# One decoder block on one core: the router's hand-written order, the place of the gate2 rows and the load of final_g

## Chip, cores and metric

The kernel runs on 1 core of one Trainium2 chip. The metric is the device time of one launch in microseconds (us), less is better. The core has five instruction queues that run beside each other: PE (TensorE; its weight loads are listed as PEld), DVE (VectorE), ACT (ScalarE), POOL (GpSimd) and SP (SyncE, here only an issuer of DMAs).

## What is computed

256 tokens of width 1024 go through a mixing layer (two kinds of attention), a hierarchical mixture of experts and a last RMSNorm, all in float32. The part that matters here is the second half:

```python
x = x + gate1 * (merged @ w_out[l])
h2 = rmsnorm(x, norm2_g[l]) * (1.0 + scale2) + shift2
y = hierarchical_moe(h2, router_group_w[l], ...)     # top-1 of 4 groups, then top-2 of its 4 experts
x = x + gate2 * y
return rmsnorm(x, final_g)
```

There are 16 experts (gate and up: 1024x512 each, down: 512x1024). The vectors shift, scale and gate come from a small product with the conditioning vector.

## The kernel before

The 256 tokens are two token tiles of 128 (t = 0, 1); a row of 1024 is two halves of 512 (n = 0, 1). Names as (t, n) below.

**w_out and the router.** `wo_steps` accumulates `merged @ w_out` in PSUM. For the second half (n = 1) tile 0 is finished first, tile 1 some microseconds later. `x1_half(t, n)` (L943) does three DVE operations that add the residual and an ACT square that gives the row sum `ss2`. `rstd2(t)` makes 1/rms of it in two POOL operations (L249, L250). `h2_half` (L997, DVE) forms h2. `q_transpose` (L956) transposes on PE and copies out with ACT. `token_logits` (L916, PE) and `fold` (L905: a copy of the logits out of PSUM, then a small PE matmul) give the router logits, `weigh_logits` (L1022, DVE) finishes them in `lg`. h2 is kept as a high part (`h2_hi`, L1009, an ACT cast to fp32r) and a low part (`h2_lo`, L1012, DVE). `seed` (L986, PE) puts the residual into the four output accumulators `oacc`. From `lg`, nine small DVE operations make `selb`, three small PE matmuls `rk` (L1085 to L1087) rank the tokens of each expert, DVE makes `pos` and the `onehot` selection, and `gather` (L1212) is 32 PE matmuls that collect each expert's tokens. `keep_clock` (L171) issues PE matmuls whose result nobody reads.

The order of all this on PE, DVE and ACT is what the text of the program says: it stands in a `manual_schedule` block, where each of these engines takes its instructions in the order in which they are written, and an engine whose next instruction waits does nothing else.

**Experts.** They run in 8 pairs. For a pair: 32 `gps` matmuls (gate), 32 `ups` (up), silu and product on ACT and DVE, `slot_weights`, `act_transpose`, and the `dps` matmuls (down) of the pair before; `weigh` scales the result by `adaacc[5]`, the rows of gate2, and `scatter` adds it to `oacc` by a matmul. In pair 0 `mod_rows(5)` (L472, two PE matmuls and two ACT copies) spreads the gate2 rows over the partitions. Weights are streamed by DMAs on SP's queue into 1 MB tiles of a ring; a DMA waits until PE has read the tile that it replaces.

**End.** After the last pair's `gps` and `ups`, `final_row` (L1132) spreads `final_g` over the partitions: a DMA of 4 KB into `fgrow` (L1129, ACT's queue, issued in the router), 8 matmuls of 8 rows in PE (16 instructions) and two ACT copies into `fg`. Then come the scatter of pair 6, the down matmuls and scatters of pair 7 in three column parts (`PARTS`: 512, 256 and 256 columns), and `norm_part` for each. `norm_end` (L1166) adds the sums of squares of both token tiles, takes the power -1/2 on POOL, scales on ACT and DVE, and writes the result in four DMAs of 256 KB, two from ACT's queue and two from SP's.

Of the kernel before, what the change touches and what calls it, by code (L numbers as in the profile page):

```python
# [13 lines left out]
ALU = mybir.AluOpType  # L14
# [3 lines left out]
P = 128  # L18
# [43 lines left out]
def hybrid_block_kernel(  # L62
# [409 lines left out]
    def mod_rows(which):  # L472

        for j in range(2):
            ps = psa(f"bc{which}{j}")
            if which == 5:
                PE.matmul(ps, ones, adaacc[which, j], start=True, stop=True)
            else:
                for i, part in enumerate(msplit[which][j]):
                    PE.matmul(ps, selr if (which, j) in ON_PE else onesr, part, start=(i == 0),  # L480
                              stop=(i == 1))
            if which == 4:
                V.scalar_tensor_tensor(adaacc[4, j], ps, 1.0, norm2[0][:, 512 * j:512 * j + 512],
                                       op0=ALU.add, op1=ALU.mult)
            else:
                S.copy(adaacc[which, j], ps)
# [601 lines left out]
    h2_lo(0, 1)  # L1088
    keep_clock(4)
# [38 lines left out]
    fgrow = small.tile([P, P], F32, name="fgrow", tag="lgs")[0:KD, :]  # L1128
    nc.scalar.dma_start(fgrow, final_g.rearrange("(k p) -> k p", p=P))  # L1129
    fg = []  # L1130

    def final_row():  # L1132

        fg.append(st.tile("fg")[:, 0:D])
        for n in range(2):
            ps = psa(f"fg{n}")
            for k in range(4):
                PE.matmul(ps[:, k * P:(k + 1) * P],
                          ident[0:KD, 4 * n + k:4 * n + k + 1].broadcast_to([KD, P]), fgrow,
                          start=(k == 0), stop=True, skip_group_check=True)  # L1140
            S.copy(fg[0][:, 512 * n:512 * n + 512], ps)

    norm = {}

    def norm_part(i):
# [7 lines left out]
        for t in range(NT):  # L1153
# [3 lines left out]
            if c is not PARTS[-1]:  # L1157
                V.tensor_tensor(o[:, t, c], oacc[t][n][:, cs], fg[0][:, c], op=ALU.mult)
# [7 lines left out]
    def norm_end():  # L1166
        o, ss = norm["o"], norm["ss"]
        c, cs = PARTS[-1], slice(PARTS[-1].start - FW, FW)
        r = small.tile([P, NT], F32, name="rstdf", tag="rstd")
        V.tensor_tensor(r, ss[:, len(PARTS) - 1, :], ss[:, len(PARTS) - 2, :], op=ALU.add)  # L1170
        G.tensor_tensor(r, r, mhalf, op=ALU.pow)
        for t in range(NT):
            rt_ = r[:, t:t + 1]
            S.mul(o[:, t, 0:512], o[:, t, 0:512], rt_)
            V.scalar_tensor_tensor(o[:, t, c], oacc[t][1][:, cs], rt_, fg[0][:, c], op0=ALU.mult,  # L1175
                                   op1=ALU.mult)
            V.tensor_scalar(o[:, t, 512:c.start], o[:, t, 512:c.start], rt_, None, op0=ALU.mult)  # L1177
            nc.scalar.dma_start(out[t * P:(t + 1) * P, 0:512], o[:, t, 0:512])
            nc.sync.dma_start(out[t * P:(t + 1) * P, 512:], o[:, t, 512:])
# [170 lines left out]
    for n in range(2):  # L1350
        h2_lo(1, n)
# [4 lines left out]
    with tc.manual_schedule(engines={PE.engine}):  # L1356
        gather(0, 0)
        gather(0, 1)
        for p in range(NP):
# [17 lines left out]
            if p == 0:  # L1377
                mod_rows(5)
# [11 lines left out]
        final_row()  # L1390
# [16 lines left out]
    norm_end()  # L1407
# [99 lines left out]
```

## Time and profile before

| | |
|---|---|
| time, median of 3 runs | 470.38 us (468.78 to 470.97) |
| the profiled execution | 470.29 us, of which the span from first to last instruction is 468.6 us |
| busy PE / PEld / DVE / ACT / POOL | 448.2 (96%) / 281.2 / 220.6 / 160.6 / 14.7 us |
| router, from the end of w_out to the first expert matmul | about 224.9 to 240.7 us |
| expert pairs | 240.7 to 441.2 us |
| last pair's down, norm, output | 441.2 to 468.6 us |

In a row of the trace the first two numbers are the start and the length in us; then come engine, line, operation, result and operands without buffer numbers, shape and count. A bracket at the end tells how long the engine had stood idle and what ended that. A float32 matmul is two instructions, so that "x4" there are two matmuls of the program. The granted clock is that of PE, 1.00 for 2.4 GHz and 0.50 for 1.2 GHz.

### The profile page before, as it was taken

To read this page: it belongs to the slowest core of one execution; us is meant where nothing else is said; L and a number is where in the kernel's file an instruction comes from. 1 tells how busy PE (TensorE), PEld (TensorE's weight loads), DVE (VectorE), ACT (ScalarE), POOL (GpSimd) and SP (SyncE) were. 2 spreads that over 40 slices of the span, in tenths; PEclk is the share of its full clock that TensorE was granted. 3 is DMA by queue.
4 is the path that set the end of the run, shared out by engine and by line. 5 is a ranking of instruction groups with operands and counts; after the bars stand their busy time and mean duration, and the time that the engine had idled before them with its cause. 6 is when DMAs were issued, how large, how long until landed. Compare 5 with 4: busy or idle time off the path is not lost. (4 is left out here: it accounts for less than half of the span.)

```text
span 468.6 us, 6867 instructions
## 1 busy us (share of the span) xinstructions
PE 448.2 (96%) x2724; PEld 281.2 (60%) x2724; DVE 220.6 (47%) x378; ACT 160.6 (34%) x292; POOL 14.7 (3%) x51
## 2 busy tenths in 40 slices
PE   5999999999999999999899999999999999999991
PEld 1769988976889999978453345333533335333440
DVE  5558878956999964787640030031202111020332
ACT  3543686465663444363641012011201102110222
POOL 5210000000000000000100000000000000000000
PEclk9999999999999999999999999999999999999986
DMA  8999978789797979976779999999999999999502
GB/s 290 368 324 354 295 267 287 247 287 382 254 374 255 385 263 407 422 308 219 294 258 408 424 420 418 422 419 421 420 421 419 422 419 421 420 420 404 196 0 94
DMA packets 51971, 158.46 MB, mean 338 GB/s; under 512 B 6448, under 2 KB 16728, under 8 KB 40160
## 3 DMA queue, kind: packets, MB, share of 16 engines
q1 hardware_dynamic: 51568, 157.44, 87.6%
q8 instruction: 23, 0.38, 0.3%
q10 hardware_dynamic: 368, 0.55, 0.3%
q14 instruction: 12, 0.10, 0.1%
HBM read 156.93 MB, written 1.05 MB: 337 GB/s over the span
## 5 line engine op out<-in xcount | busy, mean ns | idle before, releaser
L1252 PE MATMUL gps<-g,hg 128*64 128x512 f32 x256 | 57.9, 596 | 0.0
L1252 PE MATMUL ups<-u,hg 128*64 128x512 f32 x256 | 56.6, 595 | 0.0
L1309 PE MATMUL dps<-d,aT 128*64 128x512 f32 x224 | 51.2, 598 | 0.0
L1281 DVE TENSOR_TENSOR act<-act,ups 128x512 f32<-128x512 f32 x8 | 5.5, 687 | 93.6 <-PE ups L1252 93.6
L409 PE MATMUL g_acc<-hT,wsp 128*128 128x256 f32 x384 | 48.4, 285 | 0.3 <-DVE wsp L363 0.3
L409 PEld LDWEIGHTS g_acc<-hT,wsp 128*128 128x128 f32 x384 | 46.7, 191 | 1.6 <-issue 1.0
L1252 PEld LDWEIGHTS ups<-u,hg 128*64 128x64 f32 x256 | 17.9, 137 | 35.3 <-issue 35.3
L1252 PEld LDWEIGHTS gps<-g,hg 128*64 128x64 f32 x256 | 17.4, 137 | 33.2 <-issue 32.6
L1309 PEld LDWEIGHTS dps<-d,aT 128*64 128x64 f32 x224 | 14.8, 136 | 25.4 <-issue 25.2
L446 DVE SCALAR_TENSOR_TENSOR adarow<-adaw,cact,adarow 128x512 f32<-128x512 f32 x40 | 29.6, 743 | 0.4
L1327 ACT CAST yh<-yt 128x512 fp32r<-128x512 f32 x15 | 9.3, 618 | 56.7 <-DVE yt L1323 56.7
L1267 ACT CAST sT<-st 128x256 fp32r<-128x256 f32 x8 | 3.0, 372 | 63.4 <-PE st L1264 63.4
L940 PE MATMUL wo<-wsp,mT 128*128 128x512 f32 x96 | 23.7, 400 | 0.7 <-DVE wsp L363 0.7
L878 PE MATMUL br<-oT,wsp 128*128 128x256 f32 x192 | 23.2, 282 | 0.0
L1280 ACT ACTIVATE act<-gps 128x512 f32<-128x512 f32 x8 | 4.8, 598 | 53.7 <-PE gps L1252 53.7
L878 PEld LDWEIGHTS br<-oT,wsp 128*128 128x128 f32 x192 | 23.0, 188 | 0.2 <-DVE wsp L363 0.2
L1335 DVE TENSOR_TENSOR yl<-yt,yh 128x512 fp32r<-128x512 f32 x7 | 4.8, 692 | 34.3 <-PE oacc L1343 32.4
L940 PEld LDWEIGHTS wo<-wsp,mT 128*128 128x128 f32 x96 | 17.6, 188 | 5.2 <-DVE wsp L363 1.1
L1323 DVE SCALAR_TENSOR_TENSOR yt<-dps,ws,adarow 128x512 f32<-128x512 f32 (+1 forms) x17 | 12.2, 719 | 14.3 <-PE dps L1309 8.3
L1288 DVE COPY aT<-actT 128x512 f32<-128x512 f32 x8 | 5.5, 691 | 27.0 <-PE actT L1286 27.0
L1212 PEld LDWEIGHTS hg<-onehot,h2s 128*128 128x128 f32 x128 | 15.7, 191 | 4.2 <-ACT yh L1327 2.4
L1212 PE MATMUL hg<-onehot,h2s 128*128 128x256 f32 x128 | 16.8, 287 | 1.0 <-DVE h2s L1012 0.5
(295 smaller groups left out, 679.4 us busy)
## 6 DMA issues: line engine op xcount, KB each, us to landing
g<-in_expert_w_gate SPq DMA_DIRECT2D x32, 1024.0 KB, 14.6
u<-in_expert_w_up SPq DMA_DIRECT2D x32, 1024.0 KB, 16.3
d<-in_expert_w_down SPq DMA_DIRECT2D x30, 1024.0 KB, 17.2
adaw<-in_ada_w SPq DMA_DIRECT2D x16, 1024.0 KB, 6.4
ada<-in_ada_w SPq DMA_DIRECT2D x8, 512.0 KB, 8.9
ada<-in_ada_w SPq DMA_DIRECT2D x16, 256.0 KB, 8.5
wo<-in_w_out SPq DMA_DIRECT2D x4, 1024.0 KB, 12.9
kaw<-in_w_in SPq DMA_DIRECT2D x4, 512.0 KB, 6.6
```

The source lines that it names most:

```text
L409: PE.matmul(self.acc[m // 2][:, (m % 2) * T:(m % 2 + 1) * T], w[a][:, kk, m * P:(m + 1) * P], hT[b][:, k, :], start=(k == 0 and i == 0 and ...
L446: V.scalar_tensor_tensor(acc, adaw[which, j, k // 4][:, k % 4, :], cact[:, k:k + 1], acc, op0=ALU.mult, op1=ALU.add)
L878: PE.matmul(bacc[br][m // 2][:, (m % 2) * T:(m % 2 + 1) * T], wk[a][:, 0, m * P:(m + 1) * P], oT[br][b][:, k, :], start=(k == 0 and i == 0 ...
L940: PE.matmul(acc[t][n], mT[b][:, k, t * P:(t + 1) * P], ws[k // 2][a][:, k % 2, :], start=(k == 0 and i == 0), stop=(k == KD - 1 and i == 2))
L1212: PE.matmul(ps[:, kk * T:(kk + 1) * T], h2s[t][i][:, k * P:(k + 1) * P], oh[:, t].rearrange("p e s -> p (e s)"), start=(n == 0 and kk == 0 ...
L1252: PE.matmul(ps[64 * i:64 * i + 64, :], hg[:, k, (lo + i) * CAP:(lo + i + 1) * CAP], wt[nm, p][half][i][:, k % 4, :], start=(k == 0), stop= ...
L1280: S.activation(av, in_place(gu["g", p]), AF.Silu)
L1281: V.tensor_tensor(av, av, in_place(gu["u", p]), op=ALU.mult)
L1288: V.tensor_copy(aT, ap.rearrange("p (f s) -> p f s", f=KF))
L1309: PE.matmul(ys[p, FW * n][64 * i:64 * i + 64, :], aTs[p][:, 2 * h + k, 64 * i:64 * i + 64], dt_[p, h][i][:, k, FW * n:FW * n + FW], start= ...
L1323: V.scalar_tensor_tensor(y, ps, ws, adaacc[5, n][:, cs], op0=ALU.mult, op1=ALU.mult)
L1327: S.copy(hi, y)
```

## The change

The router block is written in another order: `rstd2(0)` and the three h2 steps of (0, 0) come ahead of tile 1's `x1_half(1, 1)`; the second half of tile 0 (`h2_half(0, 1)`) comes after it; both last seeds stand behind the second fold; `keep_clock` is gone from here; three of the four low parts are made in other places. The second fold's copy is DVE's. `mod_rows(5)` moves from pair 0 to the place behind `rk`. `final_row` goes; a DMA on SP's queue, behind the last weights, reads `final_g` for all 128 partitions (512 KB). `norm_end` works by token tile, and the first half-row of tile 0 is written from SP's queue.

```diff
-    def mod_rows(which):
+    def mod_rows(which, js=(0, 1)):
...
-        S.copy(lgs[:, 0:cols.stop - cols.start], lgT[:, cols])
+        (V.tensor_copy if out == 32 else S.copy)(lgs[:, 0:cols.stop - cols.start], lgT[:, cols])
...
     x1_half(0, 1)
+    rstd2(0)
     q_transpose(0, 0)
+    h2_half(0, 0)
+    h2_hi(0, 0)
+    h2_lo(0, 0)
     wo_steps(1, ws, [(k, 1) for k in W3])
     q_transpose(0, 1)
-    rstd2(0)
-    h2_half(0, 0)
-    h2_hi(0, 0)
     q_transpose(1, 0)
+    token_logits(0)
     seed(0, 0)
-    token_logits(0)
+    fold(tok(0), 0, "lgs0")
     x1_half(1, 1)
+    rstd2(1)
+    q_transpose(1, 1)
+    seed(0, 1)
+    weigh_logits(0)
     h2_half(0, 1)
-    fold(tok(0), 0, "lgs0")
-    seed(0, 1)
-    q_transpose(1, 1)
-    weigh_logits(0)
-    rstd2(1)
-    h2_hi(0, 1)
-    h2_lo(0, 0)
     h2_half(1, 0)
-    seed(1, 0)
     token_logits(1)
     fold(tok(1), 32, "lgs1")
     h2_half(1, 1)
     h2_hi(1, 0)
+    h2_hi(0, 1)
     h2_hi(1, 1)
+    weigh_logits(1)
+    seed(1, 0)
     seed(1, 1)
-    weigh_logits(1)
-    keep_clock(3)
...
     PE.matmul(rk[:, NE:2 * NE], strictb, selv[:, 1, :], start=False, stop=True)
-    h2_lo(0, 1)
-    keep_clock(4)
+    h2_lo(1, 0)
+    mod_rows(5)
...
     one_hot(0)
-    for n in range(2):
-        h2_lo(1, n)
+    for t in range(NT):
+        h2_lo(t, 1)
...
             if p == 0:
-                mod_rows(5)
                 nmaxi = most_tokens()
...
-        final_row()
+        fg = st.tile("fg")[:, 0:D]
+        nc.sync.dma_start(fg, final_g.unsqueeze(0).broadcast_to([P, D]))
...
-        r = small.tile([P, NT], F32, name="rstdf", tag="rstd")
-        V.tensor_tensor(r, ss[:, len(PARTS) - 1, :], ss[:, len(PARTS) - 2, :], op=ALU.add)
-        G.tensor_tensor(r, r, mhalf, op=ALU.pow)
+        rs = small.tile([P, NT], F32, name="rstdf", tag="rstd")
+        last = len(PARTS) - 1
         for t in range(NT):
-            rt_ = r[:, t:t + 1]
-            S.mul(o[:, t, 0:512], o[:, t, 0:512], rt_)
-            V.scalar_tensor_tensor(o[:, t, c], oacc[t][1][:, cs], rt_, fg[0][:, c], op0=ALU.mult,
+            V.tensor_tensor(rs[:, t:t + 1], ss[:, last, t:t + 1], ss[:, last - 1, t:t + 1],
+                            op=ALU.add)
+        for t in range(NT):
+            G.tensor_tensor(rs[:, t:t + 1], rs[:, t:t + 1], mhalf[:, 0:1], op=ALU.pow)
+        for t in range(NT):
+            r = rs[:, t:t + 1]
+            S.mul(o[:, t, 0:512], o[:, t, 0:512], r)
+            V.scalar_tensor_tensor(o[:, t, c], oacc[t][1][:, cs], r, fg[:, c], op0=ALU.mult,
                                    op1=ALU.mult)
...
-            nc.scalar.dma_start(out[t * P:(t + 1) * P, 0:512], o[:, t, 0:512])
+            (nc.sync, nc.scalar)[t].dma_start(out[t * P:(t + 1) * P, 0:512], o[:, t, 0:512])
             nc.sync.dma_start(out[t * P:(t + 1) * P, 512:], o[:, t, 512:])
...
-    norm_end()
+    with tc.manual_schedule(engines={V.engine, S.engine, G.engine}):
+        norm_end()
```

The order in which three engines take their instructions shows the moves. Numbers at names tell buffers apart: `adarow_1305` and `adarow_1312` are the first and second half's shift rows, `rstd_2521` and `rstd_2560` are tile 0 and tile 1 before, `rstd_2491` and `rstd_2551` after.

DVE in the router, before, from the first `h2_half` to the last `weigh_logits`:

```order
L997 SCALAR_TENSOR_TENSOR h2a<-h2a,rstd_2521,adarow_1305 128x512
L947 TENSOR_TENSOR h2a<-wo_2446,adarow_793 128x512
L948 TENSOR_TENSOR xs<-xs,h2a 128x512
L950 TENSOR_TENSOR h2a<-xs,adarow_1228 128x512
L997 SCALAR_TENSOR_TENSOR h2a<-h2a,rstd_2521,adarow_1312 128x512
L1022 SCALAR_TENSOR_TENSOR lg<-lgp,rstd_2521,cb 128x20
L1012 TENSOR_TENSOR h2s_2325<-h2a,h2s_2324 128x512
L997 SCALAR_TENSOR_TENSOR h2a<-h2a,rstd_2560,adarow_1305 128x512
L997 SCALAR_TENSOR_TENSOR h2a<-h2a,rstd_2560,adarow_1312 128x512
L1022 SCALAR_TENSOR_TENSOR lg<-lgp,rstd_2560,cb 128x20
```

The same stretch of DVE with the change:

```order
L997 SCALAR_TENSOR_TENSOR h2a<-h2a,rstd_2491,adarow_1305 128x512
L1012 TENSOR_TENSOR h2s_2325<-h2a,h2s_2324 128x512
L947 TENSOR_TENSOR h2a<-wo_2446,adarow_793 128x512
L948 TENSOR_TENSOR xs<-xs,h2a 128x512
L950 TENSOR_TENSOR h2a<-xs,adarow_1228 128x512
L1022 SCALAR_TENSOR_TENSOR lg<-lgp,rstd_2491,cb 128x20
L997 SCALAR_TENSOR_TENSOR h2a<-h2a,rstd_2491,adarow_1312 128x512
L997 SCALAR_TENSOR_TENSOR h2a<-h2a,rstd_2551,adarow_1305 128x512
L908 COPY lgs_2574<-lgT 128x128
L997 SCALAR_TENSOR_TENSOR h2a<-h2a,rstd_2551,adarow_1312 128x512
L1022 SCALAR_TENSOR_TENSOR lg<-lgp,rstd_2551,cb 128x20
```

The low part of (0, 0) (L1012) now stands ahead of tile 1's residual (L947 to L950), tile 0's second `h2_half` behind it, and the second logits copy (L908) is DVE's.

PE before, from the last seed's end to the gather: the second `keep_clock` stands between `rk` and the first gather matmul.

```order
L1085 LDWEIGHTS strictb
L1085 MATMUL rk<-rt_selb,strictb 128x16
L1086 LDWEIGHTS onesb
L1086 MATMUL rk<-rt_selb,onesb 128x16
L1087 LDWEIGHTS strictb
L1087 MATMUL rk<-rt_selb,strictb 128x16
L171 LDWEIGHTS identb
L171 MATMUL warm<-identb 128x512
```

PE with the change, from the second fold to the gather:

```order
L910 MATMUL lgp<-fold_115,lgs_2574 128x20
L986 MATMUL oacc_2582<-xs,ident 128x512
L986 MATMUL oacc_2584<-xs,ident 128x512
L1084 LDWEIGHTS strictb
L1084 MATMUL rk<-rt_selb,strictb 128x16
L1085 LDWEIGHTS onesb
L1085 MATMUL rk<-rt_selb,onesb 128x16
L1086 LDWEIGHTS strictb
L1086 MATMUL rk<-rt_selb,strictb 128x16
L477 MATMUL bc_2605<-adarow_1597,onesr 128x512
L477 MATMUL bc_2608<-adarow_1608,onesr 128x512
L1200 MATMUL hg_2642<-onehot_2613,h2s_2324 128x256
```

Two seeds stand where `keep_clock(3)` stood and the gate2 rows (L477) where `keep_clock(4)` stood; the gather is now L1200.

SP's queue behind the last weights, before and then with the change:

```order
L1242 DMA d_1_3657<-in_expert_w_down 128x4x256
L1242 DMA d_1_3658<-in_expert_w_down 128x4x256
L1410 TENSOR_LOAD nmaxi
L1410 ISA x2
L1179 DMA out<-o 128x512 x2
```

```order
L1230 DMA d_1_3646<-in_expert_w_down 128x4x256
L1230 DMA d_1_3647<-in_expert_w_down 128x4x256
L1378 DMA fg<-in_final_g 128x1024
L1399 TENSOR_LOAD nmaxi
L1399 ISA x2
L1166 DMA out<-o 128x512
L1167 DMA out<-o 128x512 x2
```

SP has the load of `fg` in front of its last steps and three of the four output DMAs instead of two.

## Rows read from the trace of the kernel before

**Rows 1.** Waits of PE from 241 us on: engine, line, releaser, total, times, longest.

```profile
PE oacc L1343 <- DVE o L1158: 0.7, 1, 0.7
```

**Rows 2.** Windows: window, length, busy of PE, PEld, DVE, ACT, POOL; clock, DMA share, GB/s.

```profile
330.00:440.00 110.00, 110.00 (x535) 44.52 (x535) 18.10 (x26) 13.92 (x32) 0.00 (x0) 1.00 1.01 413
```

**Rows 3.** Timeline of the router, DVE, ACT and POOL.

```profile
223.62 0.75 DVE L997 SCALAR_TENSOR_TENSOR h2a<-h2a,rstd,adarow 128x512 f32<-128x512 f32 x1 [1.15 <-POOL rstd L250]
224.96 0.69 DVE L947 TENSOR_TENSOR h2a<-wo,adarow 128x512 f32<-128x512 f32 x1 [0.58 <-PE wo L940]
...
225.87 1.16 ACT L1009 CAST h2s<-h2a 128x512 fp32r<-128x512 f32 x1
...
226.41 0.69 DVE L950 TENSOR_TENSOR h2a<-xs,adarow 128x512 f32<-128x512 f32 x1
...
228.03 0.27 ACT L908 COPY lgs<-lgT 128x128 f32<-128x128 f32 x1
...
228.60 0.56 POOL L250 TENSOR_TENSOR rstd<-rstd,mhalf 128x1 f32<-128x1 f32 x1
...
228.94 1.08 DVE L1012 TENSOR_TENSOR h2s<-h2a,h2s 128x512 fp32r<-128x512 f32 x1
229.93 1.42 DVE L997 SCALAR_TENSOR_TENSOR h2a<-h2a,rstd,adarow 128x512 f32<-128x512 f32 x2
...
232.47 0.24 DVE L1022 SCALAR_TENSOR_TENSOR lg<-lgp,rstd,cb 128x20 f32<-128x20 f32 x1 [1.12 <-PE lgp L910]
```

**Rows 4.** Timeline of the router, PE alone.

```profile
229.54 0.60 PE L956 MATMUL qT<-ident,h2a 128*128 128x128 f32 x4
...
234.23 0.18 PE L1085 MATMUL rk<-rt_selb,strictb 128*128 128x16 bf16 x1 [0.20 <-DVE rt_selb L1080]
...
235.77 0.78 PE L1212 MATMUL hg<-onehot,h2s 128*128 128x256 f32 x3 [0.43 <-DVE onehot L1194]
237.08 3.73 PE L1212 MATMUL hg<-onehot,h2s 128*128 128x256 f32 x29 [0.53 <-DVE h2s L1012]
240.74 7.09 PE L1252 MATMUL gps<-g,hg 128*64 128x512 f32 x32
```

**Rows 5.** Timeline of pair 0 behind its last `ups` matmul.

```profile
254.84 0.69 DVE L1281 TENSOR_TENSOR act<-act,ups 128x512 f32<-128x512 f32 x1 [13.53 <-PE ups L1252]
...
255.27 1.96 PE L477 MATMUL bc<-adarow,onesr 128*128 128x512 f32 x4
257.18 0.60 PE L1286 MATMUL actT<-ident,act 128*128 128x128 f32 x4
```

**Rows 6.** Timeline of PE and DVE where the last pair's down begins.

```profile
437.66 3.65 PE L1309 MATMUL dps<-d,aT 128*64 128x512 f32 x16
...
441.14 0.69 DVE L1330 TENSOR_TENSOR yl<-yt,yh 128x512 fp32r<-128x512 f32 x1 [0.74 <-ACT yh L1327]
...
441.25 2.05 PE L1138 MATMUL fg<-fgrow,ident 8*128 8x128 f32 x16
443.22 0.73 PE L1343 MATMUL oacc<-yh,sT 128*128 128x512 f32 x2
...
444.38 5.26 PE L1297 MATMUL dps<-d,aT 128*64 128x512 f32 x16
```

**Rows 7.** Windows around that place, columns as in rows 2.

```profile
440.50:444.00 3.50, 3.50 (x23) 2.53 (x20) 1.44 (x2) 1.81 (x4) 0.00 (x0) 1.00 0.01 4
444.50:447.50 3.00, 3.00 (x8) 0.88 (x10) 0.69 (x1) 0.00 (x0) 0.00 (x0) 0.50 0.00 0
```

**Rows 8.** Timeline of the end.

```profile
458.47 0.20 ACT L1155 ACTIVATION_READ_ACCUMULATOR act<-oacc 128x1 f32 x1
...
459.20 0.16 DVE L1170 TENSOR_TENSOR rstdf<-ssf 128x2 f32<-128x2 f32 x1 [1.29 <-ACT act L1155]
459.44 0.70 POOL L1171 TENSOR_TENSOR rstdf<-rstdf,mhalf 128x2 f32<-128x2 f32 x1 [230.29 <-DVE rstdf L1170]
...
460.95 1.01 SPq L1179 DMA_DIRECT2D out<-o  x2
```

More of the change, by code (lines that the diff above doesn't have):

```diff
@@ L470, in mod_split @@
             msplit[which].append((hi, lo))
-    def mod_rows(which):
-        for j in range(2):
+    def mod_rows(which, js=(0, 1)):
+        for j in js:
             ps = psa(f"bc{which}{j}")
@@ L1127, in hybrid_block_kernel @@
     PARTS = [slice(0, 512), slice(512, 768), slice(768, 1024)]
[L1128 to L1134, printed above, removed]
-        for n in range(2):
[L1136 to L1141, printed above, removed]
     norm = {}
@@ L1157, in norm_part @@
             if c is not PARTS[-1]:
-                V.tensor_tensor(o[:, t, c], oacc[t][n][:, cs], fg[0][:, c], op=ALU.mult)
+                V.tensor_tensor(o[:, t, c], oacc[t][n][:, cs], fg[:, c], op=ALU.mult)
         if c is not PARTS[-1]:
@@ L1168, in norm_end @@
         c, cs = PARTS[-1], slice(PARTS[-1].start - FW, FW)
-        r = small.tile([P, NT], F32, name="rstdf", tag="rstd")
-        V.tensor_tensor(r, ss[:, len(PARTS) - 1, :], ss[:, len(PARTS) - 2, :], op=ALU.add)
-        G.tensor_tensor(r, r, mhalf, op=ALU.pow)
+        rs = small.tile([P, NT], F32, name="rstdf", tag="rstd")
+        last = len(PARTS) - 1
         for t in range(NT):
-            rt_ = r[:, t:t + 1]
-            S.mul(o[:, t, 0:512], o[:, t, 0:512], rt_)
-            V.scalar_tensor_tensor(o[:, t, c], oacc[t][1][:, cs], rt_, fg[0][:, c], op0=ALU.mult,
+            V.tensor_tensor(rs[:, t:t + 1], ss[:, last, t:t + 1], ss[:, last - 1, t:t + 1],
[6 more added lines that the diff above has]
+            V.scalar_tensor_tensor(o[:, t, c], oacc[t][1][:, cs], r, fg[:, c], op0=ALU.mult,
                                    op1=ALU.mult)
-            V.tensor_scalar(o[:, t, 512:c.start], o[:, t, 512:c.start], rt_, None, op0=ALU.mult)
-            nc.scalar.dma_start(out[t * P:(t + 1) * P, 0:512], o[:, t, 0:512])
+            V.tensor_scalar(o[:, t, 512:c.start], o[:, t, 512:c.start], r, None, op0=ALU.mult)
+            (nc.sync, nc.scalar)[t].dma_start(out[t * P:(t + 1) * P, 0:512], o[:, t, 0:512])
             nc.sync.dma_start(out[t * P:(t + 1) * P, 512:], o[:, t, 512:])
@@ L1349, in hybrid_block_kernel @@
     one_hot(0)
-    for n in range(2):
-        h2_lo(1, n)
+    for t in range(NT):
+        h2_lo(t, 1)
     combv = route_weights()
```

## The prediction

> **What bounds the kernel now.** I read the waits of PE first, then windows for clock and DMA, then the timeline at the four places that the diff touches. From the first expert matmul at 240.74 us to the end, PE waits once on something that the profile names, for 0.7 us, on DVE [rows 1]; no wait is on a DMA. In the same stretch the DMA engines are full too (share 1.01, 413 GB/s), PE is busy all the time and its clock is granted in full [rows 2]. So two chains run almost level, and the question is which one sets the end. The weights are the looser one: from 440.5 us on hardly anything moves (4 GB/s) [rows 7], while pair 7's down begins at 444.38 us and reads the last loads after 449 [rows 6]. A weight DMA waits for PE to free a tile, so if PE runs earlier the stream runs earlier with it. Hence the reading: from 240.74 on PE's instructions lie end to end, each microsecond taken off PE there should come off the end, and so should each by which the gather is earlier. Ahead of that, between 225 and 237 us, PE waits for DVE and ACT [rows 3, 4], and there the order decides.
>
> The sum is made against the profiled execution, 470.29 us (span 468.6 us), which lies 0.09 below the median of 470.38. Half a per cent, 2.35 us, is about what a measurement of this kernel can tell from no change.
>
> **The router.** I replay the new order with the durations of the old rows. h2_half(0, 0) ends at 223.62 + 0.75 = 224.37, as before. Next on DVE is the low part of (0, 0), which waits for ACT's cast: 224.4 + 1.16 = 225.6, then 1.08 more to 226.7 [rows 3]. Behind it in DVE's queue stands x1_half(1, 1), which started at 224.96 before; it now starts at 226.7, **1.7 us late**, and tile 1 hangs on it. Its three steps take 2.14 (224.96 to 226.41 + 0.69) and end at 228.8. In the old order the transposes of (1, 1) could have started at 227.1 and started at 229.54 [rows 4], because PE stood in its queue behind the first fold, and that behind ACT's copy of 228.03 [rows 3]. In the new order that fold is through before 228.8, so the transposes start at about 228.95, 0.6 earlier than before. From them to weigh_logits(1) took 232.47 - 229.54 = 2.93; what lies between (transposes, ACT copy, one seed, token_logits, the copy, the fold) is the same, only the copy is DVE's; ACT's took 0.27, and I take the same for DVE. That would give 231.9; but DVE has h2_half(1, 1) between (half of 1.42), and I take 232.05. Tile 1's rstd, old end 228.60 + 0.56 = 229.16, comes about 0.75 later, since ACT's square waits for DVE, and is in time. So the logits are 0.4 earlier, and with them rk: 233.8 instead of 234.23.
>
> Behind rk PE has the two gate2 matmuls. Their row in pair 0 is 1.96 long, and 257.18 - 255.27 = 1.91 passed from their start to that of the transposes behind them [rows 5]; a small matmul lay between, so I take 1.8. The gather then starts at about 234.0 + 1.8 = 235.8, and it doesn't stall: the low part that it waited for (0.53 us, until 237.08) now stands ahead of pos, the two others are wanted 2 us later. Before, 3 of 32 matmuls came first, then the wait; 29 took 237.08 to 240.74, 0.126 each, so without the wait it would have had to start at 237.08 - 3 x 0.126 = 236.7 to end as it did. Gain: **0.9 us**. Bounds: if the whole 1.7 of the late x1_half reached the gather, it would start at 235.77 + 1.7 = 237.5, a loss of 0.8; if PE could start with onehot 0.4 earlier than its 235.77, a gain of 1.3. I stay with 0.9, because the old trace shows that the transposes had 2.4 us to spare.
>
> **Pair 0.** The gate2 matmuls go from where PE has no gap. act is ready at 254.84 + 0.69 = 255.53; its transposes started at 257.18 [rows 5] and can now start at about 255.63. Gain: **1.55 us**. ACT's two copies move too, in front of the first hg copy, and are done by about 236.4, before that one is wanted at 236.8.
>
> **final_row.** Its matmuls held PE from 441.25 to 443.22, where the scatter of pair 6 begins [rows 6]. That scatter's high half is ready at once; its low half needs yl, ready at 441.14 + 0.69 = 441.83, and the high half covers 0.57 of the time until then. Gain: 1.97 less about 0.07, **1.9 us**. The load that replaces it is 512 KB, 1.3 us at 413 GB/s [rows 2], last in SP's queue behind the weights. It is first read in norm_part, after the 16 matmuls that end at 449.6 [rows 6], some 445.7 with all gains; the stream runs dry about 440 and the load ends it near 441. Four more microseconds would cost nothing. Its ring tile was last read by a down matmul of pair 5, long before. SP's later steps wait for the end anyway.
>
> **The clock.** While final_row ran the clock was 1.00; from 444.5 to 447.5 it is 0.50 [rows 7], that is the lower level, 1.2 GHz, and the 16 down matmuls of pair 7 take 5.26 where the 16 of pair 6 took 3.65 [rows 6]. This is the only fall between 240 and 459 us. What differs just before it is two microseconds of matmuls with 8 rows and 128 columns; without them PE goes from dps through a scatter to dps. I expect the clock to stay: **1.6 us**; bounds 0 (it falls just the same) and 1.6.
>
> By the Trainium skill (TensorE: Matmul & The Clock Gate, "Why this matters for your kernels") a clock drops when PE idles between bursts. PE is busy in all of 440.5 to 444.0 [rows 7], so here row and rule differ; by the rule final_row would not be the cause, the fall would come again, and the sum would be 1.6 higher.
>
> **norm_end.** Tile 0's row sum is there at 458.47 + 0.20 = 458.67, but its add waited for tile 1's and ran at 459.20; the power of two columns took 0.70 and ended at 460.14 [rows 8]. Split, tile 0's add runs at 458.7 and its power of one column, 0.56 as in [rows 3], ends at about 459.5; tile 1's ends at about 460.1. ACT and DVE start on tile 0 some 0.6 earlier, and tile 1 follows without a gap. The output issues, 460.95 to 461.96 [rows 8], move 0.5 to 0.6 forward; three of four on SP, at a third of a microsecond each, still fit. Gain: **0.55 us**; bounds 0 and 0.65.
>
> The Trainium skill (SBUF — State Buffer, "Who interferes with whom") has a rule against this split: a DVE operation with two SBUF inputs and a GpSimd one that reads SBUF exclude each other. By it tile 1's add would wait for tile 0's power, 0.2 to 0.3 of the gain would go, and the time be about 464.1, inside the likeliest case's own spread. The trace does not show it: DVE's low part with two SBUF inputs starts at 228.94, inside POOL's power (228.60 to 229.16), and takes 1.08 [rows 3]; the next operation follows at 229.93.
>
> The warm matmuls themselves (two stretches of keep_clock) lie in PE's waits and give nothing back.
>
> **Sum.** 0.9 + 1.55 + 1.9 + 1.6 + 0.55 = 6.5: 470.29 - 6.5 = **463.8 us**, 1.4% faster.
>
> **The rivals.**
> - *The clock falls all the same*, at the tail or for one such stretch in the router. For it: why it fell is read from one case only. Against: the rows above. Price 1.6: **465.4 us**. The rule of the Trainium skill on the clock, cited above, is this case.
> - *Tile 1 is late*: the 1.7 us on DVE reach the gather. For it: DVE is strictly in order and the low part waits for ACT. Against: 2.4 us to spare. Loses 0.8 where I have a gain of 0.9: **465.5 us**.
> - *The weight stream is the real bound*, and PE only looks full. Then pair 0, final_row and clock are hidden, and 0.9 + 0.55 remain: **468.8 us**, within half a per cent. For it: share 1.01. Against: no wait of PE on a DMA, and the stream dry at 440.5.
> - *Slower*: keep_clock did its work, and without it the clock falls to half behind rk and stays there. Place: gather and pair 0. At half clock PE's work takes twice as long, so 32 gather matmuls lose about 4.1 and the first 32 of gps 7.09 [rows 4]; together 463.8 + 11.2 = **475.0 us**. It decides once 6.5 + 2.35 = 8.85 us of such work runs at half. Against: the gate2 matmuls that stand there now are as dense as the warm ones and longer, and the one fall in this trace lasted some three microseconds.
>
> That the change does not do what it says can be left out: the order of each engine shows every move.
>
> **How the numbers follow.** Forecast 0.71; clock 0.17; tile 1 late 0.05; weight stream 0.04; slower 0.03. The range goes down to 462.6 (the router at 1.3, final_row and pair 0 each 0.1 and norm_end 0.1 better, and the runs' own scatter of half a microsecond) and up to 466.4 (clock or late tile, with norm_end's gain gone and the scatter); the weight stream, the slow case and a little of the rest are left out. Faster by over 0.5%: 0.71 + 0.17 + 0.05 = 0.93; same 0.04; slower 0.03.
>
> **What would show it.** In the new profile the first gps matmul should start at about 239.8, pair 1's 1.55 us earlier still; the scatter of pair 6 should follow dps within 0.1, the 16 down matmuls of pair 7 should take 3.65 at clock 1.00, and the last output be issued about 6.5 us before 461.96. PE should still wait for no DMA. The router step is wrong if DVE's x1_half(1, 1) starts at 226.7 and the transposes of (1, 1) later than 229.5; the clock step if a window behind 440 shows 0.50; the whole reading if PE waits on weights.

## The result and the profile after

The changed kernel takes 462.79 us in the median of 4 runs (462.62 to 463.94), beside 470.41 us of the kernel before (4 runs, 468.78 to 470.97): ratio 0.985, 95% interval 0.982 to 0.988. Run a second time, beside other kernels, it took 463.84 us against 468.94: 0.988 (0.986 to 0.990). Its profiled execution is 462.77 us with a span of 460.8, that is 7.5 and 7.8 less than before.

Some runs of either kernel take 1.4 us or more longer, at a mean granted clock that is lower by 0.003 to 0.005; in the profile of the kernel before this is one fall of some three microseconds [rows 7], and below such a run is said to have a fall.

Where the 7.8 us of span came from, place by place (the start of the work that is named, and in the last column what was newly gained there):

| place | before | after | earlier by | new |
|---|---|---|---|---|
| ahead of the change, transposes of (0, 0) | 220.14 | 220.33 | -0.19 | -0.19 |
| first `gps` of pair 0 | 240.74 [rows 4] | 239.70 | 1.04 | 1.23 |
| first `gps` of pair 1 | 257.71 | 255.13 | 2.58 | 1.54 |
| second half of pair 6's down | 437.66 [rows 6] | 435.08 | 2.58 | 0 |
| first half of pair 7's down | 444.38 [rows 6] | 439.96 | 4.42 | 1.84 |
| scatter behind it | 449.57 | 443.55 | 6.02 | 1.60 |
| first output issue on SP | 460.95 [rows 8] | 454.21 | 6.74 | 0.72 |
| end of the span | 468.6 | 460.8 | 7.8 | 1.1 |

Timeline of the changed kernel in the router, against [rows 3, 4]; a row is start, length, engine, line, operation, operands, count, and in the bracket the idle time ahead of it and what ended that:

```profile
225.76 1.11 DVE L1012 TENSOR_TENSOR h2s<-h2a,h2s 128x512 fp32r<-128x512 f32 x1 [1.19 <-ACT h2s L1009]
...
226.78 0.69 DVE L947 TENSOR_TENSOR h2a<-wo,adarow 128x512 f32<-128x512 f32 x1
...
228.99 0.74 DVE L997 SCALAR_TENSOR_TENSOR h2a<-h2a,rstd,adarow 128x512 f32<-128x512 f32 x1
...
229.06 0.80 POOL L249 TENSOR_SCALAR rstd<-ss,rstd 128x1 f32<-128x1 f32 x1 [5.10 <-ACT wo L949]
229.07 0.63 PE L956 MATMUL qT<-ident,h2a 128*128 128x128 f32 x4 [1.18 <-DVE h2a L950]
...
233.89 0.18 PE L1084 MATMUL rk<-rt_selb,strictb 128*128 128x16 bf16 x1
...
234.00 1.95 PE L477 MATMUL bc<-adarow,onesr 128*128 128x512 f32 x4
235.44 4.33 PE L1200 MATMUL hg<-onehot,h2s 128*128 128x256 f32 x32
239.70 1.51 PE L1240 MATMUL gps<-g,hg 128*64 128x512 f32 x6
```

The low part (L1012) waits for ACT, `x1_half(1, 1)` (L947) stands behind it until 226.78, and the transposes of (1, 1) follow at 229.07. The 32 gather matmuls now run without the stall of [rows 4]. In pair 0 (against [rows 5]) the transposes of act follow act within 0.05 us; only small matmuls are in between:

```profile
253.80 0.69 DVE L1269 TENSOR_TENSOR act<-act,ups 128x512 f32<-128x512 f32 x1 [13.54 <-PE ups L1240]
...
254.54 0.66 PE L1274 MATMUL actT<-ident,act 128*128 128x128 f32 x4
255.13 1.08 PE L1240 MATMUL gps<-g,hg 128*64 128x512 f32 x4
```

At the tail, against [rows 6, 7], PE alone, then a window (window, length, busy of PE, PEld, DVE, ACT, POOL; clock, DMA share, GB/s):

```profile
435.08 3.65 PE L1297 MATMUL dps<-d,aT 128*64 128x512 f32 x16
438.66 0.73 PE L1331 MATMUL oacc<-yh,sT 128*128 128x512 f32 x2
...
439.96 3.65 PE L1285 MATMUL dps<-d,aT 128*64 128x512 f32 x16
443.55 0.73 PE L1331 MATMUL oacc<-yh,sT 128*128 128x512 f32 x2
```

```profile
440.00:443.00 3.00, 3.00 (x15) 1.02 (x16) 0.80 (x2) 0.62 (x1) 0.00 (x0) 1.00 0.12 49
```

`final_row` is gone and the scatter follows; the 16 down matmuls take 3.65 instead of 5.26, at clock 1.00. PE's waits from 238 us on have one row, as before, and none on a DMA [rows 1]:

```profile
PE oacc L1331 <- DVE o L1142: 0.7, 1, 0.7
```

The end, against [rows 8]:

```profile
452.64 0.16 DVE L1156 TENSOR_TENSOR rstdf<-ssf 128x1 f32<-128x1 f32 x1 [0.78 <-ACT act L1139]
452.88 1.06 POOL L1159 TENSOR_TENSOR rstdf<-rstdf,mhalf 128x1 f32<-128x1 f32 x2 [222.37 <-DVE rstdf L1156]
...
453.15 0.16 DVE L1156 TENSOR_TENSOR rstdf<-ssf 128x1 f32<-128x1 f32 x1 [0.35 <-ACT act L1139]
453.46 1.33 ACT L1162 ACTIVATE o<-o,rstdf 128x512 f32<-128x512 f32 x2 [0.35 <-POOL rstdf L1159]
...
454.21 0.36 SPq L1166 DMA_DIRECT2D out<-o  x1
```

Tile 0's add starts 0.22 us after its row sum does (452.42), before 0.73 (458.47 to 459.20 in [rows 8]); of the 0.7 us by which the first output comes earlier, 0.5 are this, and the shorter first power is most of the rest. Then there are 1.1 us that no term of the prediction holds: from the first output issue to the end of the span it is 6.6 us, before 7.65. They lie in the last bytes of the output, as windows of 0.5 and 1 us show (columns as above), first before, then after:

```profile
465.50:466.00 0.50, 0.00 (x0) 0.00 (x0) 0.00 (x0) 0.00 (x0) 0.00 (x0) 0.50 0.05 12
466.00:466.50 0.50, 0.00 (x0) 0.00 (x0) 0.00 (x0) 0.00 (x0) 0.00 (x0) 0.50 0.04 16
466.50:467.00 0.50, 0.00 (x0) 0.00 (x0) 0.00 (x0) 0.00 (x0) 0.00 (x0) 0.50 0.00 0
```

```profile
458.00:459.00 1.00, 0.00 (x0) 0.00 (x0) 0.00 (x0) 0.00 (x0) 0.00 (x0) 0.50 0.12 37
459.00:460.00 1.00, 0.00 (x0) 0.00 (x0) 0.00 (x0) 0.00 (x0) 0.00 (x0) 0.50 0.00 0
```

Before, a remainder still trickles at 12 to 16 GB/s until about 466.4, 5.5 us behind the first issue; after, the last byte has moved by about 458.5, 4.25 us behind it.

### The profile page after: what moved, and what is told of

The parts are those of the page before. It is cut to its first block, busy times and chain, and to the rows that moved or that the text cites. A ratio compares the mean times of both kernels' runs of the same rounds, so it can differ in the third digit from the quotient of the medians.

```text
span 460.8 us, 6816 instructions
## 1 busy us (share of the span) xinstructions
PE 443.0 (96%) x2701; PEld 278.5 (60%) x2701; DVE 221.1 (48%) x380; ACT 159.6 (35%) x289; POOL 15.7 (3%) x52
## 4 chain that ended last, share of the span: by engine, by line
PE 82%; DVE 9%; DMA 4%; issue 2%; ACT 1%; POOL 0%; SPq 0%; DVEq 0%; ACTq 0%
PE gps L1240 12%; PE ups L1240 12%; PE dps L1297 11%; PE g_acc L409 7%; PE wo L940 5%; PE br L878 4%; PE oacc L1331 4%; PE hg L1200 3%; PE qb_acc L409 2%; DMA adaw<-in_ada_w 2%; PE kb_acc L409 2%; DVE adarow L446 2%; PE ka_acc L409 2%; PE va_acc L401 2%; DMA u<-in_expert_w_up 2%
## 5 line engine op out<-in xcount | busy, mean ns | idle before, releaser
L1200 PEld LDWEIGHTS hg<-onehot,h2s 128*128 128x128 f32 x128 | 15.6, 191 | 2.9 <-ACT yh L1315 2.4
L1200 PE MATMUL hg<-onehot,h2s 128*128 128x256 f32 x128 | 16.6, 288 | 0.0
```

Of the source, the lines that this page charges most:

```text
L1200: PE.matmul(ps[:, kk * T:(kk + 1) * T], h2s[t][i][:, k * P:(k + 1) * P], oh[:, t].rearrange("p e s -> p (e s)"), start=(n == 0 and kk == 0 ...
```

## The experiments

Theory: PE's instructions are the chain; each part takes its own price off the end, and the fall of the clock goes with `final_row`. Rivals: the fall has nothing to do with it; the parts do not add up; the warm matmuls were needed.

**One part alone, or one undone**

`final_g` by DMA alone, in the kernel before:

```diff
-        final_row()
+        fg.append(st.tile("fg")[:, 0:D])
+        nc.sync.dma_start(fg[0], final_g.unsqueeze(0).broadcast_to([P, D]))
```

> The kernel before with one part of the change: final_g comes by the DMA of 512 KB, final_row's 16 matmul instructions and its two copies are gone, all else stays. Theory (PE's instructions lie end to end, and the fall of the clock goes with final_row): the 1.9 us of final_row and 1.6 us of clock come off, 470.3 - 3.5 = 466.8 us; the scatter of pair 6 follows the down matmuls within 0.1 us, the 16 down matmuls of pair 7 take 3.65 us instead of 5.26, the window behind them shows clock 1.00. Rival, the clock falls all the same: 468.4 us, and the 16 take about 5.26 again. Rival, the weight stream is the bound: 470.3 us, with PE waiting for a DMA in pair 7.

466.96 us against 470.29, ratio 0.994 (0.992 to 0.996). PE in its profile:

```profile
441.32 0.73 PE L1329 MATMUL oacc<-yh,sT 128*128 128x512 f32 x2
...
442.62 3.65 PE L1283 MATMUL dps<-d,aT 128*64 128x512 f32 x16
```

The scatter starts 1.9 us earlier than in [rows 6], the 16 take 3.65: the theory's time and rows. But one of its six runs is 469.02 us with a mean clock of 0.988, and the kernel before has on that chip 4 of 11 runs at 468.8 to 469.2 us with 0.991 or 0.992, and 7 at 470.2 to 471.1 with 0.989. So, by time and mean clock, the kernel before has the fall in some of its runs only.

The gate2 rows alone, in the kernel before:

```diff
     h2_lo(0, 1)
-    keep_clock(4)
+    mod_rows(5)
...
             if p == 0:
-                mod_rows(5)
```

> The kernel before with one part of the change: the two gate2 matmuls (mod_rows(5)) stand behind rk in the place of the second keep_clock, and no longer in pair 0. Theory: in the router they lie in PE's time up to 237.08, where the gather waits for a low part anyway, so they cost nothing, and pair 0 loses 1.55 us: 468.7 us, the transposes of act start about 0.1 us after act. Rival, the gather starts later behind them and pushes its 32 matmuls: a gain of 1.2 or less, 469.1 us or more, the first gps matmul after 240.9. Rival, the weight stream is the bound behind pair 0: 470.3 us.

467.36 us, ratio 0.994 (0.992 to 0.996); all six runs lie between 467.21 and 467.42. Beside the 469.0 us of the runs of before that have no fall this is 1.6, the price of pair 0; in the router the rows hide in the gather's stall, as the theory has it. (In its profile the first `gps` is at 240.98, which looks like the rival's; but the transposes of (0, 0), ahead of the edit, are 0.23 later too than before, at 220.37.) PE, the second part of the gather, `final_row` and the down matmuls:

```profile
237.33 3.72 PE L1212 MATMUL hg<-onehot,h2s 128*128 128x256 f32 x29 [0.47 <-DVE h2s L1012]
...
439.96 2.05 PE L1138 MATMUL fg<-fgrow,ident 8*128 8x128 f32 x16
...
443.06 3.65 PE L1297 MATMUL dps<-d,aT 128*64 128x512 f32 x16
```

Here `final_row` is in the kernel, and the 16 down matmuls behind it still take 3.65. So `final_row` alone does not make the clock fall.

The old `norm_end` in the changed kernel:

```diff
-        for t in range(NT):
-            V.tensor_tensor(rs[:, t:t + 1], ss[:, last, t:t + 1], ss[:, last - 1, t:t + 1],
-                            op=ALU.add)
-        for t in range(NT):
-            G.tensor_tensor(rs[:, t:t + 1], rs[:, t:t + 1], mhalf[:, 0:1], op=ALU.pow)
+        V.tensor_tensor(r, ss[:, len(PARTS) - 1, :], ss[:, len(PARTS) - 2, :], op=ALU.add)
+        G.tensor_tensor(r, r, mhalf, op=ALU.pow)
...
-            (nc.sync, nc.scalar)[t].dma_start(out[t * P:(t + 1) * P, 0:512], o[:, t, 0:512])
+            nc.scalar.dma_start(out[t * P:(t + 1) * P, 0:512], o[:, t, 0:512])
...
-    with tc.manual_schedule(engines={V.engine, S.engine, G.engine}):
-        norm_end()
+    norm_end()
```

> The changed kernel with the old norm_end (one add and one power for both token tiles, both first half-rows written from ACT's queue). The changed kernel gained 1.4 us behind the last output issue that no term of the prediction holds. Theory A, that 1.4 us belongs to the division by token tile (outputs that start earlier and lie on the queues in another way): undoing costs 0.4 + 1.4 = 1.8 us, 464.6 us, and the time from the last issue to the end is about 6.6 us again. Theory B, it is the spread from one run to the next, or comes from elsewhere in the change: undoing costs 0.4 to 0.65 us, 463.2 to 463.5 us, and that time stays near 5.3 us.

The hand-written order around `norm_end` goes too and was not tried apart. 466.12 us in the median, ratio 0.990 (0.988 to 0.992), more than either theory has. The profile says why for its run: 1.9 us are lost long before the change, at 29 us. PE's waits up to 40 us, and two windows:

```profile
PE adat L336 <- DVE aacc L330: 1.6, 1, 1.6
```

```profile
26.00:29.00 3.00, 1.36 (x11) 1.25 (x11) 2.99 (x6) 1.04 (x1) 0.00 (x0) 0.99 1.10 349
29.00:32.00 3.00, 3.00 (x11) 2.52 (x10) 1.65 (x6) 1.77 (x3) 0.00 (x0) 0.50 1.14 286
```

PE stood 1.6 us for DVE, and then the clock was 0.50, the level of 1.2 GHz; in the profile of the changed kernel this wait is not there. Four of the six runs are 465.98 to 466.28 us; the two others, 464.31 and 464.34, are 1.5 above the 462.8 of the changed kernel, nearer to theory A's 1.8 than to theory B's 0.4 to 0.65. In the profile 7.5 us lie between first output issue and end, and the trickle is back, until 5.25 us behind the first issue. That speaks for theory A: the new end carries the 1.1 us behind the issue too.

The old router order in the changed kernel (all lines of the router's diff taken back but for the gate2 rows; the part around `rk`):

```diff
-    weigh_logits(1)
-    seed(1, 0)
     seed(1, 1)
+    weigh_logits(1)
+    keep_clock(3)
...
-    h2_lo(1, 0)
+    h2_lo(0, 1)
     mod_rows(5)
```

> The changed kernel with the router in the old order, keep_clock(3) and ACT's copy included; the gate2 matmuls stay behind rk. Theory: the new order is worth 1.0 to 1.2 us, with the first gps matmul at about 240.7 to 240.9 instead of 239.70, and the gather's stall on a low part until about 237.1 is back: 464.0 us. Rival, the order is worth nothing, and the gain in the router came from the gate2 rows in keep_clock's place: 462.8 us, the first gps matmul at 239.7. Rival, the loss is larger because gate2 rows and stall add up: the first gps matmul after 241.2, 464.5 us or more.

464.81 us, ratio 0.988 (0.987 to 0.990); the profiled run 463.84. The stall is back, and the first `gps` at 240.86 instead of 239.70:

```profile
237.19 3.74 PE L1201 MATMUL hg<-onehot,h2s 128*128 128x256 f32 x29 [0.45 <-DVE h2s L1012]
240.86 1.08 PE L1241 MATMUL gps<-g,hg 128*64 128x512 f32 x4
```

So the order is worth 1.16 us. The median says 2.0, but four of the six runs (464.78 to 465.01) are about 1.1 longer than the two others with no fall of the clock (0.994 to 0.996). No profile shows where these 1.1 us lie.

**The fall of the clock**

Full rows at the place of `final_row`, in the kernel with `final_g` by DMA:

```diff
+        for n in range(2):
+            ps = psa(f"full{n}")
+            for k in range(4):
+                PE.matmul(ps[:, k * P:(k + 1) * P],
+                          ident[:, 4 * n + k:4 * n + k + 1].broadcast_to([P, P]), ident,
+                          start=(k == 0), stop=True, skip_group_check=True)
         scatter_pair(p - 1, 0, whole_cols[0])
```

> The kernel before with final_g by DMA (as in the run with that alone), and in final_row's place 16 float32 matmul instructions of the same columns with 128 rows where final_row's have 8; their result is not read. They should take about 2 us and start at about 441.3 as final_row did, so this stretch and its moment are final_row's, only the rows differ. Theory, 8-row matmuls bring the fall of the clock: no fall here, 467.0 + 2.0 = 469.0 us, dps of pair 7 3.65 us. Rival, the moment in the program or the shortness of these matmuls brings it, whatever their rows: the fall comes in a good part of the runs as it does before, and the median is 470.4 us with the 16 down matmuls at 5.3 us and a clock of 0.50 behind 444.

468.72 us against 468.94 of the kernel before on that chip. Three of its 12 runs are 470.6 to 470.7 us with a mean clock of 0.989 or 0.990; the kernel before has 6 such in 23. In its profile nothing falls:

```profile
441.40 2.05 PE L1381 MATMUL full<-ident 128*128 128x128 f32 x16
...
444.31 3.65 PE L1283 MATMUL dps<-d,aT 128*64 128x512 f32 x16
```

So 12 runs show no difference between 8 rows and 128; that the few rows bring the fall is not supported.

The kernel with only the gate2 rows moved, and `final_row` at its old moment:

```diff
+        keep_clock(6)
         final_row()
```

> The kernel of the run with only the gate2 rows moved (467.36 us, final_row in it, and no fall of the clock in its profile), with six warm bf16 matmuls (about 1.3 us) put ahead of final_row, so that final_row begins at 441.25 us again, as in the kernel before. Theory, final_row's moment decides whether the clock falls: the fall is back in a good part of the runs, 467.4 + 1.3 + 1.6 = 470.3 us, the others at 468.7. Rival, the clock falls behind final_row by chance and whenever it stands: some runs fall and some do not, but the run without warm matmuls should then have shown it too. Rival, the warm matmuls ahead of final_row keep the clock up: 468.7 us in every run.

468.72 us, three of 12 runs at 470.0 to 470.4 (0.989). In its profile `final_row` starts at 441.27 and the 16 down matmuls take 3.65. That is the kernel before's share on this chip (6 of 23). The same kernel without the six warm matmuls had no fall in six runs, on a chip where the kernel before had 7 of 11. It leans to the moment, and is too few runs to settle it.

`final_row`'s matmuls back into the changed kernel (with the old output queues, see below):

```diff
+                PE.matmul(ps[:, k * P:(k + 1) * P],
+                          ident[0:8, 4 * n + k:4 * n + k + 1].broadcast_to([8, P]), ident[0:8, :],
+                          start=(k == 0), stop=True, skip_group_check=True)
         scatter_pair(p - 1, 0, whole_cols[0])
```

> The changed kernel with the old output queues (462.65 us), and in final_row's old place its 16 PE instructions of 8 rows again, their result unread; the load by DMA stays. Theory, they cost their own length less what the scatter waits anyway: 1.9 us, 464.5 us, and no more, with the 16 down matmuls of pair 7 at 3.65 us. Rival, they bring the fall of the clock with them: 466.1 us, 5.3 us for the 16. Rival, the load by DMA is what the clock needs or suffers from, not the matmuls: 464.5 us without a fall, which then cannot be told from the theory by this run alone.

465.45 us, ratio 0.990 (0.988 to 0.992). The two shortest runs, 464.26 and 464.47, are 1.6 to 1.8 above 462.65: the length of the matmuls. The profiled run, 465.97, has the fall again behind them, here 2.7 us earlier than in the kernel before:

```profile
438.56 2.05 PE L1382 MATMUL unread<-ident 8*128 8x128 f32 x16
...
441.66 5.35 PE L1285 MATMUL dps<-d,aT 128*64 128x512 f32 x16
```

```profile
442.00:445.00 3.00, 3.00 (x10) 0.91 (x8) 0.53 (x1) 0.00 (x0) 0.00 (x0) 0.50 0.00 0
```

So the moment 441.25 is not needed either. Counting as a fall a run 1.4 us or more above its kernel's shortest with a mean clock lower by 0.003 or more: the kernel before 20 of 51; with such a stretch elsewhere or with full rows 7 of 36 (gate2 rows moved 0 of 6, the same with warm matmuls 3 of 12, full rows 3 of 12, the last one 1 of 6); with nothing there 4 of 39 (the changed kernel 1 of 10, `final_g` by DMA 1 of 6, old router 0 of 6, the changed kernel with the old output queues and its two router variants below 2 of 17). The old `norm_end` has 3 of 6, but its profiled fall is the one at 29 us; the kernel without warm matmuls, next, is left out, since its clock falls in the router. 7 of 36 and 4 of 39 can't be told apart by so few runs. Where the falls of runs without a profile lie is not known.

The kernel before without its warm matmuls:

```diff
-    keep_clock(3)
...
-    keep_clock(4)
```

> The kernel before without its two stretches of warm matmuls in the router (keep_clock(3) and keep_clock(4)), and nothing else. Theory: PE waits there anyway and its clock stays at 1.00 behind, 468.9 us beside 468.9 us, with the gather at its old place. Rival, the one that the prediction gave for slower: without them the clock falls to 0.50 behind rk, the gather and the first gps matmuls lose up to 11 us: 472 to 480 us, a granted clock of 0.50 in a window between 236 and 248.

471.91 us, 469.72 to 475.04 in 12 runs, against 469.00: ratio 1.006 (1.003 to 1.008). The rival is right that the clock falls, and the theory wrong; the median lies just under the rival's 472 to 480 us. Windows of the kernel before in the router, then of this one:

```profile
232.00:234.00 2.00, 1.97 (x7) 0.82 (x7) 1.40 (x10) 1.99 (x2) 0.00 (x0) 1.00 1.01 426
234.00:236.00 2.00, 1.37 (x10) 0.61 (x9) 1.97 (x6) 0.00 (x0) 0.00 (x0) 1.00 1.04 399
236.00:239.00 3.00, 2.47 (x19) 2.17 (x19) 2.98 (x8) 0.95 (x2) 0.00 (x0) 1.00 0.88 363
```

```profile
232.00:234.00 2.00, 1.35 (x4) 0.52 (x4) 1.36 (x9) 2.00 (x3) 0.00 (x0) 1.00 0.99 401
234.00:236.00 2.00, 0.32 (x4) 0.25 (x5) 1.93 (x6) 0.05 (x1) 0.00 (x0) 1.00 1.03 424
236.00:239.00 3.00, 2.65 (x11) 2.36 (x12) 3.00 (x8) 0.32 (x1) 0.00 (x0) 0.52 0.81 336
```

PE is busy 0.32 us in the two ahead of 236, then the clock is 0.52 and the gather's 29 matmuls take 4.77 instead of 3.73. None of the 12 runs has a mean clock above 0.989. The profiled run is the shortest of the 12; where the others lose up to 5.3 us more is not shown. In the changed kernel the gate2 rows stand in that gap (PE busy 2.00 of 2.00 from 234 to 236), and the clock is 1.00 behind it. That they keep it there is likely by this; no run takes them out of the changed kernel.

**The end**

The changed kernel again:

> The changed kernel once more, unchanged, beside the others on the same chip, for the spread that its time has. From its four runs: 462.7 us in most, about 463.9 in one of four. If the fall of the clock is gone for good, no run has the mean clock of 0.989; if the end's 1.4 us that the prediction lacks is a matter of chance, the runs fall into two groups 1.1 to 1.4 us apart.

462.73 to 465.12 us in six runs: 462.73, 463.31, three at 463.78 to 463.91, and one at 465.12 with the lowest clock (0.989). So runs with no fall differ by up to 1.2 us. The profiled one, 463.31, has 7.05 us between first output issue and end; its last byte moves as early as in the profile above (4.25 us behind the first issue), and the 0.45 us lie behind that. Of the other runs this is not known.

The old output queues:

```diff
-            (nc.sync, nc.scalar)[t].dma_start(out[t * P:(t + 1) * P, 0:512], o[:, t, 0:512])
+            nc.scalar.dma_start(out[t * P:(t + 1) * P, 0:512], o[:, t, 0:512])
```

> The changed kernel with only the output queues as before: tile 0's first half-row from ACT's queue, so two output DMAs on ACT and two on SP; adds, powers and order stay. Theory, the 1.2 us that the new end gained behind the last output issue come from the third DMA on SP's queue (one early output instead of two pairs issued at once): undoing it gives 1.0 to 1.3 us back, 463.9 us, the wait for the outputs' landing on SP grows from 3.5 to about 4.8 us. Rival, they come from tile 0's outputs being issued earlier through the split add and power: 462.7 to 462.9 us, and that wait stays near 3.5 us.

462.65 us, ratio 0.987 (0.984 to 0.989); five of six runs lie between 462.55 and 462.66 and one, at 465.94, has a lower clock. The rival is right: the gain does not come from the third DMA on SP. It issues like this:

```profile
454.18 0.40 ACTq L1166 DMA_DIRECT2D out<-o  x1
454.20 1.00 SPq L1167 DMA_DIRECT2D out<-o  x2
...
455.38 0.37 ACTq L1166 DMA_DIRECT2D out<-o  x1
```

From the first output issue to the end of the span it is 7.3 to 7.7 us in the seven profiles with the old `norm_end`, 6.6 to 7.05 in the three with the new one and three outputs on SP, and 6.4 in the four with the new one and two outputs on each queue. The bulk of the 1 MB goes at the same rate (365 to 397 GB/s before, 365 to 389 after, over 2.5 us). What differs is the trickle behind it: in all seven profiles with the old `norm_end` the last byte moves 5.25 to 5.5 us behind the first issue, in all seven with the new one 4.25.

That outputs issued tile by tile land and end sooner than four at once is shown, also with the old queues. Why the four leave a trickle is not.

**The router's order, and POOL beside DVE**

The low part of (0, 0) behind `x1_half(1, 1)` (old output queues):

```diff
     h2_hi(0, 0)
-    h2_lo(0, 0)
...
     x1_half(1, 1)
+    h2_lo(0, 0)
     rstd2(1)
```

> The changed kernel with the old output queues (462.65 us), and in the router DVE's low part of (0, 0) behind tile 1's x1_half(1, 1) instead of ahead of it, so that x1_half no longer waits for ACT's cast. Theory, the 1.7 us by which x1_half(1, 1) came late now do cost: replayed with the durations of the changed kernel, x1_half starts at 225.2 instead of 226.78, the transposes of (1, 1) at 227.9 instead of 229.07 (now behind the fold of tile 0), and tile 1's logits, rk and the first gps matmul come 0.95 us earlier (gps at 238.75): 461.7 us. Rival, the chain is held elsewhere (ACT's copies, POOL's rstd(1) slowed by the low part beside it): gps at 239.4 or later, 462.4 to 462.7 us. Rival, slower: rstd(1) comes so late that weigh_logits(1) waits for it, 463 us.

461.55 us (461.52 to 461.64 in five runs) against 469.00, ratio 0.983 (0.980 to 0.985), and 1.1 below the same kernel with the low part ahead: faster than both kernels. DVE, POOL and PE:

```profile
225.06 0.69 DVE L947 TENSOR_TENSOR h2a<-wo,adarow 128x512 f32<-128x512 f32 x1 [0.58 <-PE wo L940]
...
227.66 0.63 PE L956 MATMUL qT<-ident,h2a 128*128 128x128 f32 x4
227.69 0.61 POOL L249 TENSOR_SCALAR rstd<-ss,rstd 128x1 f32<-128x1 f32 x1 [3.81 <-ACT wo L949]
...
228.38 1.06 POOL L250 TENSOR_TENSOR rstd<-rstd,mhalf 128x1 f32<-128x1 f32 x1
...
238.57 2.80 PE L1240 MATMUL gps<-g,hg 128*64 128x512 f32 x12
```

`h2_half(0, 1)` behind `h2_half(1, 0)` (old output queues):

```diff
-    h2_half(0, 1)
     h2_half(1, 0)
+    h2_half(0, 1)
```

> The changed kernel with the old output queues (462.65 us), and in the router h2_half(0, 1) behind h2_half(1, 0). In the changed kernel the first POOL step of rstd(1) took 0.80 us beside h2_half(0, 1), which reads two operands from SBUF on DVE, and 0.27 us elsewhere. Theory, the two shut each other out: with no DVE operation beside it that step takes 0.27 us again, rstd(1) is ready about 0.5 us earlier; but the second logits copy on DVE now stands behind two halves, so the time is 462.6 to 462.9 us. Rival, the step is slow for another reason: it takes 0.80 us again, and the time is 463.2 us, since h2_half(0, 1) then lies in front of the copy.

462.74 us, ratio 0.986 (0.984 to 0.989): no difference from 462.65. But POOL's step is short again, since DVE has nothing to do beside it:

```profile
228.99 0.27 POOL L249 TENSOR_SCALAR rstd<-ss,rstd 128x1 f32<-128x1 f32 x1 [5.09 <-ACT wo L949]
```

The same step takes 0.27 with DVE idle, 0.80 beside `h2_half(0, 1)` in the changed kernel, 0.61 beside the low part in the run above; there the power (0.56 elsewhere) also takes 1.06, beside `h2_half(0, 1)` (228.26 to 229.01).

## Why the prediction was right, and where not

Predicted 463.8 us (462.6 to 466.4), measured 462.79, near the lower end of the range. Where the time would go was right in router, pair 0 and final_row; the clock's term came true in the two profiles, but its cause was not borne out, and the end's term was too small.

- **Router**, 0.9 predicted, 1.23 measured (1.16 by undoing it). The replay held: x1_half at 226.78 (226.7), `weigh_logits(1)` at 232.13 (232.05), `rk` at 233.89 (233.8), no stall. The gather came at 235.44, not 235.8: I had given the two gate2 matmuls 1.8 us of PE, and 1.44 passed from their start to the gather's. One sentence there misleads, that the transposes had 2.4 us to spare: that was true of the old order, in which PE waited for the first fold. In the new order that fold is early and the late `x1_half` costs 1.1 us, as the run with the low part behind it shows.
- **Pair 0**, 1.55 predicted, 1.54 in the profile, 1.6 alone. The gate2 rows cost nothing in the router, since the PE gap they fill was there already.
- **final_row**, 1.9 predicted, 1.84 in the profile, 1.9 alone, 1.6 to 1.8 put back. The DMA that replaces it made nobody wait.
- **The clock**, 1.6 predicted. In the two profiled executions it is 1.60, but the step "what differs just before it is two microseconds of matmuls with 8 rows" failed as a cause: three profiles have `final_row` and no fall behind it (gate2 rows moved, the same with warm matmuls, no warm matmuls in the router), full rows go with as many falls, and the kernel before has a fall in 20 of 51 runs only. Without any such matmuls there a fall is rarer (4 of 39); but the variants with them have 7 of 36 only, and the kernel before ranges from 6 of 23 on one chip to 7 of 11 on another, so how much is due to `final_row`, and why one run falls and the next doesn't, stays open. So the term is no 1.6 us of each run. Between runs without a fall the change is worth 468.9 - 462.7 = 6.2 us, which is about router 1.2, pair 0 1.55, final_row 1.9 and norm_end 1.5 to 1.8 (against 463.8, where half of the repeated runs lie, it is 5.1). The median before, 470.4, had the fall in it because most of its few runs did.
- **norm_end**, 0.55 predicted for the output issues, 0.72 found for the first of them. The mis-sized step is "the output issues move 0.5 to 0.6 forward" taken as all there is: behind the issue another 1.1 us went, in the last bytes of the output. It comes with the split by tile, not from the queue. The third output on SP is no help: with two on each queue five of six runs lie closer (462.55 to 462.66).
- **The slower rival** did not come, but its mechanism is real: without the warm matmuls and with nothing in their place the clock falls to 0.52 in the router and the kernel is 2.9 us slower. "As dense as the warm ones and longer", the reason given against it, fits: behind the gate2 rows the clock is 1.00.
- **Weight stream**: PE still waits for no DMA; right.

That the sum came out near is partly luck: the clock's 1.6 was counted as sure and is missing in many runs, and 1.1 us of the end and 0.3 of the router were not counted.

## What to carry to other kernels

A fall of the clock in one profile is one run: look at the spread and mean clock of all runs before counting it into a sum. Warm matmuls in a gap can be replaced by useful matmuls of the same length, but not just dropped. On an engine that takes its work in order, put what waits for another engine behind the head of the longer chain; and let the last reduction end tile by tile, so that the first outputs leave early.

## What the runs showed of the hardware that was not expected

- DVE does hold POOL up. In the prediction I held against the rule (the Trainium skill, SBUF — State Buffer, "Who interferes with whom": a DVE operation with two SBUF inputs and a GpSimd one that reads SBUF contend) that a low part took 1.08 inside POOL's power [rows 3]. That row was weak: DVE began 0.34 us into a POOL operation of 0.56. Where POOL starts beside such a DVE operation, its step takes 0.61 to 0.80 instead of 0.27, and 1.06 instead of 0.56: the trace agrees with the rule. That POOL holds DVE up no run shows: the low part that began inside POOL's power was no longer than others (1.07 to 1.11). In `norm_end` it cost nothing: tile 1's add took its 0.16 inside tile 0's power.
- The clock falls after PE has stood: 1.6 us of waiting ahead of the 0.50 at 29 us, 0.32 us busy of 2.00 ahead of the 0.52 at 236. The Trainium skill (TensorE: Matmul & The Clock Gate, "Why this matters for your kernels") has it that idle gaps between bursts of matmuls bring the clock down; these two falls agree in kind, though the waits were shorter than the gap it names. The falls at 444 us [rows 7] and, with the matmuls put back, at 442 us came with PE busy in all of the three microseconds before; that rule does not explain them.
- The load of `final_g` for 128 partitions held SP's queue for 2.12 us, a weight load 0.33; nobody waited for it.
- Four output DMAs of 256 KB, issued within 1.0 us, left a trickle in the kernel before: 12 to 16 GB/s, a share of 0.04 to 0.05, in the last microsecond of the 5.5 that they took. Issued tile by tile they were through in 4.25.
